# Dot products of the modulation's last eight columns move from the FFN's input norm into the mLSTM's stream

## Chip, cores, metric

The kernel runs on one core of one Trainium2 chip. The metric is the device time of one launch in microseconds (us), the median of three timed runs. The engines are named as in the profile: PE (TensorE, matmuls), DVE (VectorE), ACT (ScalarE), POOL (GpSimd), SP (SyncE, which issues nearly all DMA transfers).

## What is computed

One encoder layer for 1024 tokens of width 1024 in float32. Of it, what matters here:

```python
cond = jax.nn.silu(c)
mod = cond @ w_ada[l] + b_ada[l]
sh1, sc1, g1, sh2, sc2, g2 = jnp.split(mod, 6, axis=-1)
h = modulate(rms_norm(x, norm_mix_g[l]), sh1, sc1)
proj = h @ w_in[l]
...
mix = jnp.concatenate([y_attn, y_mem], axis=-1) @ w_out[l]
x = x + g1[:, None, :] * mix
h = modulate(rms_norm(x, norm_ffn_g[l]), sh2, sc2)
ffn = (jax.nn.silu(h @ w_gate[l]) * (h @ w_up[l])) @ w_down[l]
x = x + g2[:, None, :] * ffn
return rms_norm(x, final_norm_g)
```

`mod` has 6 x 1024 values, kept as 48 columns of 128: columns 0 to 15 are sh1 and sc1, 16 to 39 are g1, sh2 and sc2, and 40 to 47 are g2. g2 is used only where the FFN's output is added, at the end of the layer.

## The kernel before

**Modulation.** A column of `mod` is a dot product of 128 rows of the transposed `w_ada` with `cond`, done on DVE: `cond` (silu of c) lies in all partitions, a half row tile `ada` (128x512, 256 KB) is loaded, and one `scalar_tensor_tensor` multiplies it by `cond` and sums along the row into `modacc`. On the chip that is two instructions, the product and a `DVE_READ_ACCUMULATOR`. `ada_late(last, ahead)` issues the next half column (there are 64 halves for columns 16 to 47), as long as fewer than `ahead` are under way; after the last it calls `mod_sum(40, 48)`, two small additions.

**Stages.** (1) norm 1 and columns 0 to 15; (2) the input projection and the attention, with columns 16 to 39; (3) the mLSTM: four heads, each with state sums (`states`, tiles U, Cs), scores (`front`, tiles E, W), numerators (`back`, na, ni, num) and an end (`last`, `transposed`, tiles hs, ss, dn), as four streams on PE; the rest of the projection (matmuls into `acct`, evacuated by ACT as `vstg`) and then the output projection (`out_unit`, "o" units of the attention and "m" units of the mLSTM) fill PE between them; (4) the last "m" units, whose sums are added into the residual stream by DVE (`x<-acc,mod,x`), squared by ACT (`sq`) and summed by DVE (`ssq`); PE then sums over partitions (`ms`), ACT and DVE make the reciprocal root (`ny`, `nv`), DVE multiplies (`x<-x,ny`), ACT modulates, and ACT, DVE and POOL split the result into high and low parts (`h111h`, `h111l`, ...) and into their sums for the FFN; (5) the FFN in Winograd's form, gate and up, then down; (6) the last norm.

**What sets the order.** All engines' instructions are written in one pass in Python. `Clock` holds the expected end of each engine's work; `Clock.streams` takes the first PE stream that is ready by these expected times, so each expected cost on DVE, ACT, POOL or DMA moves where PE's instructions stand in their order. Once written, every engine works through its own list in order. SP issues DMA transfers in the order of the list too, and an issue that waits for its tile to be free holds up the issues behind it.

Before the change, `cond` is loaded a second time and columns 40 to 47 are made in stage 4, beside the output projection's last units:

```python
        cond_ok = load_cond(PP["ada"])
        ck.streams([un], stop=lambda: cond_ok.done and ada_late(64, 4))
        while not summed:
            ck.need(*adas[-2:])
            ada_late(64, 4)
```

Every vector, scalar and GpSimd instruction goes through the helper `Engine`, so all of them have line 96 in the profile and are told apart by their tiles. Matmuls of three parts (high x high, high x low, low x high) are lines 295 to 297, DMA issues line 300.

Of the kernel before, what the change touches and what calls it, by code (L numbers as in the profile page):

```python
# [20 lines left out]
P = 128  # L21
S = 1024
D = 1024
# [46 lines left out]
class Flag:  # L70
    """done: what sets it is emitted; t: when that is expected to end"""
# [12 lines left out]
class Engine:  # L84
    """An engine's instructions with their expected times."""
# [39 lines left out]
class Clock:  # L125
    """Emits instructions in the order of expected times (us), each engine's in the order in which they are ready."""

    def __init__(self):
        self.t = self.now = self.fin = self.dma_t = self.dma_q = 0.0
        self.q = []  # L130
        self.n = 0
        self.free = {"act": 0.0, "dve": 0.0, "gps": 0.0}
        self.table = "exp"

# [8 lines left out]
    def chain(self, delay, *steps, flag=None, bg=None):  # L143
        """Functions that follow one another. bg: the engine of each step; the step waits until that is idle."""
# [24 lines left out]
    def dma(self, nbytes, issue):  # L169
        """delay until a transfer that is issued now has arrived"""  # L170
# [9 lines left out]
    def need(self, *flags):  # L180
        """What sets the flags is emitted before what follows."""
        for f in flags:
            while not f.done:
                self.pop()
            self.until(f.t)
# [10 lines left out]
    def add_pe(self, dt):  # L196
        """work of the tensor engine that is not a stream's"""
# [7 lines left out]
    def streams(self, mains, fills=(), stop=None):  # L205
        """Runs streams, the first that is ready first, until the mains have ended or stop() holds."""
        every = [*mains, *fills]
        while any(s.wait is not None for s in mains) and not (stop and stop()):
            s = next((s for s in every if s.ready() <= self.t), None)
            if s:  # L210
                s.go()
# [9 lines left out]
class Stream:  # L221
    """A part of the tensor engine's work: a generator that yields the flags that its next piece needs."""
# [15 lines left out]
def layer_kernel(ctx, tc, xT, c, w_ada, vecs, cons, rope, w_f, w_t0, w_t, w_o, w_gu, w_d, out):  # L238
# [8 lines left out]
    # ---------------------------------------------------------------- constants  # L247
# [23 lines left out]
    # DRAM scratch  # L271
# [39 lines left out]
    def psum_open(name, tags, bufs=1):  # L311
        """tags: name -> (tag, buffers)"""
# [7 lines left out]
    class slot:  # L320
        """what frees the next tile of a tag"""
# [26 lines left out]
    with tc.manual_schedule():  # L348
# [12 lines left out]
        def load_cond(pool):  # L361
            """silu of c, the same for all partitions"""
# [11 lines left out]
        # ---------------------------------------------------- weights in a ring of six pieces  # L374
# [46 lines left out]
        def raw(shape, src, flag, arrived):  # L421
            """a transfer into the ring of three; flag: it has been used; arrived(tile, delay)"""
# [10 lines left out]
        def split(p, delay, src, shape, *before, lo=None):  # L433
            """the parts of a piece"""
# [12 lines left out]
        def piece(i):  # L447
            """a piece; its transfer, where it has one of its own"""
# [11 lines left out]
        def load_piece():  # L460
            """the next piece, once there is room for it"""
# [17 lines left out]
        # ---------------------------------------------------- norm 1, modulation, first three tiles  # L479
# [13 lines left out]
        for k in range(KT):  # L493
            def sum_up(k=k):
                """adds a tile's squares"""
# [34 lines left out]
        def rstd_steps(ms, scale, tag, put, flag=None):  # L530
            """1/sqrt(scale*ms + eps), with one Newton step"""
# [25 lines left out]
        def h_steps(k):  # L557
            """the modulated norm of a tile and its parts"""
# [22 lines left out]
        def h_when(k):  # L581
            """starts a tile when its columns of the modulation are there"""
# [26 lines left out]
        # ---------------------------------------------------- q and k: gain, mean square, rotation  # L609
# [6 lines left out]
        def rope_steps(i, accs):  # L616
            """i: q tile 0..3, or 4 for k"""
# [77 lines left out]
        # ---------------------------------------------------- units of the projection  # L695
# [3 lines left out]
        def tile_mms(w0, last):  # L699
            """two halves of a tile of features; last(n, acc, flag) when half n is summed"""  # L700
# [26 lines left out]
        def conv_unit(i, w0):  # L727
# [19 lines left out]
            def silu():  # L747
                """2*silu(y) = y*(1 + tanh(y/2))"""
# [60 lines left out]
        # ---------------------------------------------------- gate rows: fw heads at 0..3, bw heads at 32..35  # L809
        def gate_steps():  # L810
# [100 lines left out]
            def decay():  # L911
                # decay of a chunk: exp(rend + mprev), spread over all partitions
# [19 lines left out]
        def ada_late(last=48, ahead=2):  # L932
            """the next half of a column of the modulation that is not needed at once"""
# [1127 lines left out]
```

## Time and profile before

| | us |
|---|---|
| median of 3 timed runs | 1436.59 |
| lowest, highest | 1433.66, 1437.8 |
| span of the profiled execution, first to last instruction | 1431.8 |
| PE busy | 1310.1 (91%) |
| DVE busy | 1075.9 (75%) |
| POOL busy | 792.6 (55%) |
| ACT busy | 660.6 (46%) |

The profiled execution's own time is known by its span alone; the timed runs lie 1.9 to 6.0 us above that span, the median 4.8. Busy shares are averages over stages that have different limits, so the argument goes by stretches of the span: stage 3 is about 508 to 668 us, stage 4 about 668 to 800, the FFN from there on. A time in brackets at the end of a row is the idle time of that engine just before the instruction, and what ended it.

### The profile page before, as it was taken

What the parts mean: (1) busy time and instruction counts of PE and PEld (TensorE: products, weight loads), DVE (VectorE), ACT (ScalarE), POOL (GpSimd) and SP (SyncE); (2) the same over time, 40 slices, a digit from 0 to 9 for tenths busy, and PEclk for the clock granted to TensorE, in tenths of its full rate; (3) what the DMA queues carried; (4) which work ended last, traced back from release to release, by engine and by line L of the source; (5) the groups of instructions that cost most, each with busy time, mean ns of one, the idle gap of its engine ahead of it and who ended that gap; (6) DMA issues with size and microseconds to landing.
All of it is one profiled execution on the core that took longest, in us unless ns stands there. A gap on an engine that the chain in (4) does not pass through costs nothing.

```text
span 1431.8 us, 19550 instructions
## 1 busy us (share of the span) xinstructions
PE 1310.1 (91%) x6594; PEld 1075.7 (75%) x6602; DVE 1075.9 (75%) x1542; ACT 660.6 (46%) x1191; POOL 792.6 (55%) x624
## 2 busy tenths in 40 slices
PE   5789799999999999899877899999999999979997
PEld 2577677888878988777655688888888887757786
DVE  6947989987788836776899786766666654988676
ACT  5444326677666645454555333332333234433462
POOL 5555454444444336766557564554544444799942
PEclk9899899999999999999999999999999999999999
DMA  7446452322112144824742342232333159623324
GB/s 285 158 127 198 148 153 78 118 66 77 44 52 60 38 136 127 291 94 165 239 155 67 102 141 103 96 106 101 111 110 102 62 185 339 247 67 88 103 63 151
DMA packets 103172, 184.40 MB, mean 129 GB/s; under 512 B 11296, under 2 KB 32672, under 8 KB 103072
## 3 DMA queue, kind: packets, MB, share of 16 engines
q1 hardware_dynamic: 89968, 161.06, 35.2%
q10 hardware_dynamic: 13104, 22.10, 4.2%
q8 instruction: 52, 0.85, 0.3%
q14 instruction: 48, 0.39, 0.1%
HBM read 136.19 MB, written 43.25 MB: 125 GB/s over the span
## 4 chain that ended last, share of the span: by engine, by line
PE 55%; DVE 19%; issue 8%; DMA 7%; POOL 6%; ACT 3%; SPq 1%; DVEq 0%; POOLq 0%; ACTq 0%
PE acc L296 13%; PE acc L295 13%; PE acc L297 13%; POOL wlo L96 3%; DVE x L96 3%; DVE ada L96 3%; DVE sst L96 3%; PE av L1025 2%; DMA wst<-act_d 2%; PE T L1006 2%; DVE PT L96 2%; PE S L974 2%; DVE y L96 2%; PE acct L295 2%; PE acct L297 1%
## 5 line engine op out<-in xcount | busy, mean ns | idle before, releaser
L96 POOL TENSOR_TENSOR wlo<-wst,whi 128x512 fp32r<-128x512 f32 (+2 forms) x208 | 309.0, 1492 | 227.4 <-ACT whi L96 211.2
L96 ACT ACTIVATE whi<-wst 128x512 fp32r<-128x512 f32 (+2 forms) x219 | 131.9, 606 | 141.8 <-PE acc L297 22.4
L96 POOL TENSOR_SCALAR P<-P,sst 128x1024 f32<-128x1024 f32 x64 | 88.9, 1392 | 141.2 <-DVE sst L96 99.8
L296 PE MATMUL acc<-x,whi 128*128 128x512 f32 x352 | 139.6, 397 | 3.3 <-DVE x L96 3.3
L96 POOL TENSOR_TENSOR wlo<-wr,whi 128x512 fp32r<-128x512 f32 x60 | 83.5, 1392 | 78.3 <-ACT whi L96 74.9
L295 PE MATMUL acc<-hh,whi 128*128 128x512 f32 x224 | 97.8, 436 | 13.5 <-ACT hh L96 11.3
L297 PE MATMUL acc<-whi,wcl 128*128 128x512 f32 x244 | 98.1, 402 | 9.5 <-POOL wcl L96 9.5
L96 ACT ACTIVATE P<-S,sst,colq 128x1024 f32<-128x1024 f32 x64 | 77.3, 1207 | 52.2 <-DVE sst L96 47.8
L295 PE MATMUL acc<-whi,wch 128*128 128x512 f32 x244 | 96.8, 397 | 4.0 <-ACT wch L96 4.0
L296 PE MATMUL acc<-hl,whi 128*128 128x512 f32 x224 | 92.8, 414 | 8.2 <-POOL hl L96 4.5
L296 PE MATMUL acc<-wlo,wch 128*128 128x512 f32 x244 | 96.9, 397 | 1.1 <-POOL wlo L96 1.1
L297 PE MATMUL acc<-hh,wlo 128*128 128x512 f32 x224 | 91.5, 409 | 0.0
L96 DVE SCALAR_TENSOR_TENSOR ada<-ada,cond 128x512 f32<-128x512 f32 (+1 forms) x79 | 84.9, 1082 | 7.3 <-DMA ada<-in_w_ada_dram 7.2
L96 DVE TENSOR_TENSOR sg<-acc,sg 128x512 f32<-128x512 f32 x67 | 45.4, 687 | 59.3 <-PE acc L297 58.9
L96 ACT ACTIVATE PT<-T 128x512 fp32r<-128x512 f32 x128 | 71.4, 597 | 37.8 <-PE T L1006 37.1
L96 DVE TENSOR_TENSOR PT<-T,PT 128x512 fp32r<-128x512 f32 x128 | 82.8, 681 | 7.2 <-ACT PT L96 7.1
L96 ACT ACTIVATE whi<-wr 128x512 fp32r<-128x512 f32 x60 | 37.9, 632 | 106.1 <-DVE wr L96 49.6
L96 POOL TENSOR_TENSOR wlo<-s,whi 128x512 fp32r<-128x512 f32 x44 | 60.8, 1383 | 38.3 <-ACT whi L96 31.7
L295 PE MATMUL acct<-whi,hh 128*128 128x256 f32 (+1 forms) x256 | 79.3, 310 | 2.4 <-ACT xp L96 1.0
L296 PEld LDWEIGHTS acc<-x,whi 128*128 128x128 f32 x352 | 66.5, 189 | 19.2 <-DVE x L96 4.2
L96 DVE SCALAR_TENSOR_TENSOR x<-acc,mod,x 128x512 f32<-128x512 f32 (+1 forms) x92 | 62.7, 719 | 24.1 <-PE acc L297 24.1
L1006 PE MATMUL T<-con,P 128*128 128x128 f32 x512 | 70.2, 275 | 10.4 <-DVE PT L96 7.6
(457 smaller groups left out, 3875.1 us busy)
## 6 DMA issues: line engine op xcount, KB each, us to landing
wr<-in_w_gu_dram SPq DMA_DIRECT2D x66, 256.0 KB, 2.8
ada<-in_w_ada_dram SPq DMA_DIRECT2D x64, 256.0 KB, 3.6
wd<-in_w_d_dram SPq DMA_DIRECT2D x22, 512.0 KB, 7.0
wst<-in_w_gu_dram SPq DMA_DIRECT2D x34, 256.0 KB, 3.1
wst<-act_d SPq DMA_DIRECT2D x33, 256.0 KB, 4.1
ada<-in_w_ada_dram SPq DMA_DIRECT2D x16, 512.0 KB, 4.9
wst<-in_w_o_dram SPq DMA_DIRECT2D x32, 256.0 KB, 4.3
act_d<-sg ACTq DMA_DIRECT2D x31, 256.0 KB, 2.0
```

The source lines that it names most:

```text
L96: return fn(*args, **kw)
L295: nc.tensor.matmul(acc, w[0], x[0], start=first, stop=False)
L296: nc.tensor.matmul(acc, w[0], x[1], start=False, stop=False)
L297: nc.tensor.matmul(acc, w[1], x[0], start=False, stop=last)
L974: nc.tensor.matmul(sp[:, halves(n)], qs[:, j * P:(j + 1) * P], k2[g][m][:, halves(n)], start=m == 0, stop=m == 1)
L1006: nc.tensor.transpose(tp[:, k], Pt[q][:, (4 * b + k) * P:(4 * b + k + 1) * P], ident)
L1025: nc.tensor.matmul(av, va[:, k, h // 4], PT[it][m][:, k], start=(k, m) == (0, 0), stop=(k, m) == (NJ - 1, 1))
```

## The change

The condition is loaded, and its silu taken, at the beginning of the mLSTM (stage 3); `ada_late` is called each time `Clock.streams` lets a PE stream go on, with two halves under way at most instead of four, until the 16 halves are done; the two loops of stage 4 lose their calls. The pool of stage 4 that held `cond` and the `ada` tiles is gone; they lie in the pool `big` now. Comments and docstrings are removed as well, which changes no instruction; line numbers behind the additions shift by a few.

```diff
@@ class Clock
+        self.tick = None
...
             s = next((s for s in every if s.ready() <= self.t), None)
             if s:
+                if self.tick:
+                    self.tick()
                 s.go()
                 continue
...
@@ layer_kernel
         kvpool.__exit__(None, None, None)
-        bp = big_open(3)
+        bp = PP["ada"] = big_open(3)
+        load_cond(bp)
...
         mem = [Stream(g) for g in (ends(), backs(), fronts(), all_states())]
+        ck.tick = lambda: ada_late(64)
         ck.streams(mem, [un], stop=lambda: un.wait is None and all(f.done for v in vo_ok for f in v))
+        while not summed:
+            ck.need(*adas[-2:])
+            ada_late(64)
+        ck.tick = None
...
         psum_open("ps3", {"acc": ("acc", 8), "ms": ("acc", 8)})
-        adpool = tc.tile_pool(name="ad", bufs=1, side="right")
-        PP["ada"] = adpool.__enter__()
-        cond_ok = load_cond(PP["ada"])
-        ck.streams([un], stop=lambda: cond_ok.done and ada_late(64, 4))
-        while not summed:
-            ck.need(*adas[-2:])
-            ada_late(64, 4)
-        adpool.__exit__(None, None, None)
+        ck.streams([un])
         opool.__exit__(None, None, None)
```

How the order of instructions moves, at three places. First DVE's list at the beginning of the mLSTM, right after `mod_sum(16, 40)`; `W` are the weights of a score tile, `Cs` the states, `num` the numerators. Before:

```order
L96 SCALAR_TENSOR_TENSOR sc_5005<-mod,vec 128x8
L96 SCALAR_TENSOR_TENSOR W<-tr,W 128x256 x2
L96 SCALAR_TENSOR_TENSOR Cs<-Cs,dec,U 128x130 x4
L96 SCALAR_TENSOR_TENSOR W<-tr,W 128x256 x2
L96 SCALAR_TENSOR_TENSOR Cs<-Cs,dec,U 128x130 x3
L96 SCALAR_TENSOR_TENSOR Cs<-Cs,dec 128x130 x4
```

And with the change:

```order
L96 SCALAR_TENSOR_TENSOR sc_5007<-mod,vec 128x8
L96 SCALAR_TENSOR_TENSOR ada,modacc<-ada,cond 128x512 x3
L96 SCALAR_TENSOR_TENSOR Cs<-Cs,dec,U 128x130 x2
L96 SCALAR_TENSOR_TENSOR W<-tr,W 128x256 x2
L96 SCALAR_TENSOR_TENSOR ada,modacc<-ada,cond 128x512
L96 SCALAR_TENSOR_TENSOR Cs<-Cs,dec,U 128x130 x2
L96 SCALAR_TENSOR_TENSOR W<-tr,W 128x256 x2
L96 SCALAR_TENSOR_TENSOR ada,modacc<-ada,cond 128x512 x2
L96 SCALAR_TENSOR_TENSOR Cs<-Cs,dec,U 128x130 x3
L96 SCALAR_TENSOR_TENSOR Cs<-Cs,dec 128x130 x2
L96 SCALAR_TENSOR_TENSOR ada,modacc<-ada,cond 128x512
```

Three products stand ahead of the first state update and the rest between updates; the sixteenth stands before the second head's third state update, and from there on DVE's list in the mLSTM holds none.

Second, SP's list at the same place, from the first load of the mLSTM on (`mq`, `mk`, `v` are a head's q, k and v, `wst` weights). Before:

```order
L300 DMA mq<-mqk_d_85 128x256
L300 DMA mk<-mqk_d_89 128x1024
L300 DMA v_5017<-v_d_93 128x8x128
L300 DMA v_d_94<-vstg 128x256 x2
L300 DMA wst<-in_w_t_dram 128x512 x2
```

And with the change:

```order
L303 DMA cond<-in_c_dram 128x1024
L303 DMA ada<-in_w_ada_dram 128x512
L303 DMA mq<-mqk_d_85 128x256
L303 DMA ada<-in_w_ada_dram 128x512
L303 DMA mk<-mqk_d_89 128x1024
L303 DMA v_5023<-v_d_93 128x8x128
L303 DMA v_d_94<-vstg 128x256
L303 DMA wst<-in_w_t_dram 128x512
L303 DMA ada<-in_w_ada_dram 128x512
L303 DMA wst<-in_w_t_dram 128x512
```

The condition and two halves are issued ahead of the head's k and v, and further halves between the weights; the third half's issue waits for the first product to free its tile.

Third, DVE's list in stage 4, from the sum of squares after the first reciprocal root to the low part `h113l` that PE needs. Before:

```order
L96 TENSOR_TENSOR x_6177<-x_6177,ny 128x512
L96 SCALAR_TENSOR_TENSOR x_5973<-acc,mod,x_5973 128x512
L96 TENSOR_TENSOR h111l<-x_6071,h111h 128x512
L96 SCALAR_TENSOR_TENSOR ada,modacc<-ada,cond 128x512 x2
L96 SCALAR_TENSOR_TENSOR x_5982<-acc,mod,x_5982 128x512
L96 SCALAR_TENSOR_TENSOR ada,modacc<-ada,cond 128x512
L96 TENSOR_TENSOR ssq<-ssq,sq 128x512
L96 TENSOR_TENSOR mod<-modacc,vec 128x8
L96 TENSOR_TENSOR mod<-mod,modacc 128x8
L96 SCALAR_TENSOR_TENSOR x_6008<-acc,mod,x_6008 128x512
L96 TENSOR_TENSOR h113l<-x_6099,h113h 128x512
```

And with the change:

```order
L96 TENSOR_TENSOR x_6234<-x_6234,ny 128x512
L96 SCALAR_TENSOR_TENSOR x_6033<-acc,mod,x_6033 128x512
L96 TENSOR_TENSOR h111l<-x_6122,h111h 128x512
L96 SCALAR_TENSOR_TENSOR x_6045<-acc,mod,x_6045 128x512
L96 TENSOR_TENSOR ssq<-ssq,sq 128x512
L96 TENSOR_TENSOR h113l<-x_6168,h113h 128x512
```

The products and the two additions of `mod_sum(40, 48)` are gone from between the norm's steps; one addition of a tile's sum (`x<-acc,mod,x`) that stood ahead of `h113l` now stands behind it.

## Rows read from the trace of the kernel before

**Rows 1.** The page: span, and the busy time of each engine.

```profile
span 1431.8 us, 19550 instructions
...
PE 1310.1 (91%) x6594; PEld 1075.7 (75%) x6602; DVE 1075.9 (75%) x1542; ACT 660.6 (46%) x1191; POOL 792.6 (55%) x624
```

**Rows 2.** Busy time by stretch: from and to, length, then busy us (and instructions) of PE, PE's weight loads, DVE, ACT and POOL, the granted clock of PE, the share of the DMA engines, GB/s. The last line is of the FFN.

```profile
508.00:520.00 12.00, 10.20 (x78) 9.38 (x79) 1.05 (x4) 2.68 (x8) 1.91 (x9) 1.00 0.61 196
520.00:540.00 20.00, 19.94 (x145) 18.85 (x145) 10.44 (x32) 11.13 (x34) 10.82 (x21) 1.00 0.41 124
540.00:560.00 20.00, 19.89 (x148) 18.82 (x149) 11.58 (x30) 12.41 (x33) 15.32 (x26) 1.00 0.38 120
...
600.00:620.00 20.00, 16.20 (x85) 13.83 (x86) 16.06 (x34) 7.91 (x22) 11.80 (x17) 0.91 0.45 147
...
640.00:660.00 20.00, 19.74 (x103) 16.36 (x103) 16.45 (x36) 9.35 (x23) 14.11 (x11) 1.00 0.42 138
...
720.00:740.00 20.00, 13.01 (x43) 9.51 (x42) 17.77 (x28) 8.83 (x15) 6.82 (x5) 0.83 0.56 185
...
760.00:780.00 20.00, 14.40 (x46) 10.05 (x44) 20.00 (x18) 8.84 (x17) 15.04 (x10) 0.83 0.13 42
780.00:800.00 20.00, 12.57 (x43) 9.18 (x44) 15.18 (x16) 8.36 (x16) 15.47 (x11) 0.83 0.28 90
...
900.00:1000.00 100.00, 100.00 (x435) 81.38 (x434) 67.22 (x79) 31.08 (x50) 50.14 (x37) 1.00 0.31 106
```

**Rows 3.** DVE's groups of one shape: count, busy us, mean ns of one, idle us before them. The first line is of the stretch 675 to 730, the second of 698 to 730, the last two of 520 to 560 and of 560 to 600.

```profile
L96 DVE SCALAR_TENSOR_TENSOR ada<-ada,cond 128x512 f32<-128x512 f32 x16 | 17.7, 1118 | 0.1
...
L96 DVE SCALAR_TENSOR_TENSOR ada<-ada,cond 128x512 f32<-128x512 f32 x8 | 9.8, 1230 | 0.0
...
L96 DVE SCALAR_TENSOR_TENSOR Cs<-Cs,dec 128x130 f32<-128x130 f32 x7 | 2.5, 353 | 0.3 <-ACT Cs L96 0.2
...
L96 DVE SCALAR_TENSOR_TENSOR Cs<-Cs,dec 128x130 f32<-128x130 f32 x8 | 8.2, 1021 | 0.3
```

**Rows 4.** The chain of work that ended last, in the stretch 686 to 730 (44 us): shares of the stretch by engine, tile and line. "issue" is time in which the engine waited for nothing that the profile shows.

```profile
by line: DVE x L96 22.0%; DVE ada L96 21.4%; DVE ssq L96 17.7%; issue 13.7%; PE acc L296 5.2%; PE ms L1159 4.7%; PE acc L295 3.5%; PE acc L297 3.5%; ACT sq L96 2.9%; DVE ny L96 1.6%; DVE nv L96 1.6%; DVE h113l L96 1.4%; DVE h111l L96 1.4%; 
```

**Rows 5.** What PE waited for in the stretch 695 to 735: us in total, times, longest.

```profile
PE acc L296 <- DVE h113l L96: 4.7, 1, 4.7
PE ms L1159 <- DVE ssq L96: 3.3, 1, 3.3
PE acc L296 <- DVE h111l L96: 2.3, 1, 2.3
```

**Rows 6.** PE's instructions in order of time (start, us, what) around these waits. There are eleven matmuls between the last two lines.

```profile
691.57 0.39 PE L297 MATMUL acc<-yah,wlo 128*128 128x512 f32 x1
695.26 2.08 PE L1159 MATMUL ms<-ssq,ones 128*128 128x512 f32 x2 [3.30 <-DVE ssq L96]
...
719.87 0.39 PE L295 MATMUL acc<-h110h,whi 128*128 128x512 f32 x1
...
724.53 0.40 PE L295 MATMUL acc<-h113h,whi 128*128 128x512 f32 x1
729.62 0.79 PE L296 MATMUL acc<-h113l,whi 128*128 128x512 f32 x1 [4.69 <-DVE h113l L96]
730.21 0.63 PE L297 MATMUL acc<-h113h,wlo 128*128 128x512 f32 x1
...
735.29 0.39 PE L297 MATMUL acc<-h113h,wlo 128*128 128x512 f32 x1
```

**Rows 7.** DVE's and ACT's instructions in order of time, in stage 4.

```profile
692.85 0.74 DVE L96 SCALAR_TENSOR_TENSOR x<-acc,mod,x 128x512 f32<-128x512 f32 x1
...
693.68 0.63 ACT L96 ACTIVATE sq<-x 128x512 f32<-128x512 f32 x1 [3.51 <-DVE x L96]
...
694.52 0.68 DVE L96 TENSOR_TENSOR ssq<-ssq,sq 128x512 f32<-128x512 f32 x1
...
701.94 0.75 DVE L96 SCALAR_TENSOR_TENSOR x<-acc,mod,x 128x512 f32<-128x512 f32 x1 [1.44 <-PE acc L297]
...
728.88 0.68 DVE L96 TENSOR_TENSOR h113l<-x,h113h 128x512 fp32r<-128x512 f32 x1
...
739.36 0.69 DVE L96 TENSOR_SCALAR nv<-ms 128x512 f32<-128x512 f32 x1 [2.20 <-ACT ny L96]
```

**Rows 8.** The beginning of the mLSTM in order of time: PE's first transposition of k, and DVE's first work after 508.3.

```profile
515.63 0.41 PE L1675 MATMUL tr<-con,mk 128*128 128x128 f32 x2 [1.43 <-issue]
...
518.76 0.76 DVE L96 SCALAR_TENSOR_TENSOR W<-tr,W 128x256 f32<-128x256 f32 x2 [10.43 <-DMA v_d<-vstg]
```

**Rows 9.** What PE waited for on DVE in the mLSTM; the first line is of the stretch 508 to 580, the second of 600 to 668.

```profile
PE ni L1787 <- DVE num L96: 1.8, 2, 1.0
...
PE ni L1787 <- DVE num L96: 5.5, 2, 3.7
```

**Rows 10.** The silu of the condition on ACT in stage 4, with the table load ahead of it, and the transfer of the condition: KB, us from issue to landing.

```profile
673.88 1.28 ACT L96 ACT_TABLE_LOAD   x1
675.18 1.06 ACT L96 ACTIVATE cond<-cond 128x1024 f32<-128x1024 f32 x1
...
cond<-in_c_dram SPq DMA_DIRECT2D x1, 512.0 KB, 4.6
```

## Prediction

> **What bounds the kernel now.** The page comes first: PE is busy for 91% of 1431.8 us [rows 1], so most of the span is PE's. The busy times by stretch say where it is not [rows 2]. In the FFN (900 to 1000) PE is busy all the time: what stage 4 gains or loses reaches the end unchanged. In the first part of the mLSTM (520 to 560) PE is busy 39.8 of 40 us, DVE 22.0, so PE bounds and DVE has 18 us to spare. In stage 4 it is the other way round: PE is busy 13.0, 14.4 and 12.6 us in the three stretches of 20 from 720, 760 and 780, DVE 17.8, 20.0 and 15.2, and PE's granted clock is 0.83 there. The chain that ended last agrees: between 686 and 730 two thirds is DVE, and 21.4% of these 44 us, **9.4 us**, are the sixteen products' own [rows 4]. Their mean there is 1118 ns [rows 3]. The change takes them out of that place.
>
> **What it takes out of stage 4.** Sixteen products, 17.7 us of DVE [rows 3], their accumulator reads, a table load and the silu on ACT, 1.28 and 1.06 us [rows 10], and 4.7 MB of transfers. I look at it from PE and from DVE.
>
> From PE: it waited 2.3 us for `h111l` and 4.7 for `h113l` [rows 5]. DVE worked without a gap from 701.94 to the end of `h113l` at 729.56, 27.6 us [rows 7]. Of the eight products between 698 and 730 seven lie in this stretch, at the mean of 1.23 us 8.6 [rows 3]. Without them `h113l` ends at 701.94 + 19.0 = 720.9, and PE asks for it at about 724.8, after the matmul that starts at 724.53 [rows 6]. Both waits, **7.0 us**, go, with almost 4 us to spare; the change also puts one addition of a sum behind `h113l`. After the second wait the twelve matmuls from 730.21 to 735.29 took 0.63 us each at first against 0.39 at the end [rows 6]: PE ran at 1.2 instead of 2.4 GHz, and half of these 5.1 us, **2.5**, comes back if PE doesn't stop. The wait of 3.3 us before `ms` shrinks little: the last sum of the unit ahead ends at 691.96, the addition, the square and the addition of squares need 0.74 + 0.63 + 0.68 = 2.05 [rows 6, 7], with some 0.3 between them 694.3 instead of 695.26, **1.0**. PE's sum is 10.5.
>
> From DVE: the chain's 9.4 us go, but the two products ahead of `ms` (about 2.7 of them) give only the 1.0 just worked out, since PE's last sum then sets the time: 9.4 - 2.7 + 1.0 = **7.7**. From 739.36, where DVE starts on the second root after an idle time of 2.2 us [rows 7], to about 793 DVE sets the pace [rows 2], so the smaller sum counts. Above it stands up to 1.4 more, the wait of DVE for PE at 701.94 [rows 7], if PE's slow clock after `ms` goes too. I take **8**, with 5 and 11 as bounds: 5 if POOL's work, freed of DVE's, moves so that other DVE instructions meet it, 11 if PE's sum is reached.
>
> The transfers freed from 674 to 726 and the table load cost the path nothing now: PE's waits there are on DVE alone [rows 5].
>
> **What it adds to the mLSTM.** The products take DVE time from about 514 on, in DVE's list until the second head's third state update. That is about 555 in the trace of before. DVE is busy 1.05 us in 508 to 520 and 22.0 in 520 to 560 [rows 2]; with 17.7 it would be 41 of 52. PE has the projection's matmuls to fill with, but PE's list is fixed, so a state or numerator that is late by more than the list allows stops PE, with everything behind it. Price: where DVE was busy 16.1 and 16.5 of 20 us, in 600 to 660, about as full as it will be here, PE waited 5.5 us for `num`; at half the load, 1.8 in 72 us [rows 2, 9]. The order was written with the products' expected time in it, so the lists already give way. Two or three microseconds of new waits are near the middle of these rows. Against that stands a gap that closes: PE waited 1.43 us ahead of the first transposition of k [rows 8], and the changed list has 24 more projection matmuls in front of it, at 145 matmuls in 19.94 us [rows 2] about 3.3 us of work, which are merely done earlier. Net I take **1 us lost**; the bounds are a gain of 1.4 and a loss of all 19 us of DVE time.
>
> The condition's transfer and its silu: SP issues them ahead of the head's k and v. The condition took 4.6 us to land [rows 10]; issued at about 508.3, where DVE's idle time of 10.4 us begins [rows 8], it has its silu done by about 514, ahead of the 518.76 at which DVE starts. One half (256 KB) ahead of k and v costs 1.3 us at the 196 GB/s of this stretch [rows 2]; the 3.3 us of projection matmuls cover it. What this costs if that cover is gone is the 1.3 us. ACT gets the silu and two table loads, 1.06 + 2 x 1.28 = 3.6 us, in a stretch where it is busy 2.7 of 12 [rows 2, 10]; behind it waits the evacuation of the two `acct` sums, with PE behind that. I cost it at nothing, 1 us at most.
>
> On the table load page and trace differ. The row has the silu start 1.30 us after the load began, so a load costs 1.3 [rows 10]. The Trainium skill, "ScalarE: Activation LUTs", section "What ACT_TABLE_LOAD costs", adds a drain of about 1.38 us to the 1.28, some 2.66 for each switch. By that, ACT would be held 6.4 us instead of 3.6 at the beginning of the mLSTM, PE would stop for its two sums, and the sum would be about 2.8 us worse; the trace shows no such drain.
>
> **Sum.** Stage 4 gives 8, the mLSTM costs 1: the span goes from 1431.8 to 1424.8. The median lies 4.8 above the span of the profiled execution, so **1429.6 us**, 0.5% faster.
>
> **Rivals.** *Slower: the mLSTM pays.* DVE's small state updates stretch when POOL works: 353 ns in 520 to 560, 1021 in 560 to 600 [rows 3]. The products, 128x512, hold DVE for 0.7 to 1.8 us at a time in the middle of the chain of states, which DVE does one after the other. If 60% of their 19 us became PE waits, 11.4, less the 8 of stage 4, that is 3.4 slower, 1440; it decides from 42% on. For it: the products' mean of 1118 ns, and that PE's list is rigid. Against it: 1.8 us of PE waits for DVE in 508 to 580, and DVE's 29 idle us of 52. The Trainium skill, "GPSIMD Engine Reference", section "Key points", says that GpSimd shares its SBUF interfaces with VectorE and contends with instructions of two SBUF inputs, as the products are; by that rule they stay slow in the new place, where POOL is busy 26 of 40 us, and POOL's own work stretches too. The two means of the state update agree.
>
> *No change: stage 4 doesn't follow.* DVE's time is given back to POOL's and ACT's: the high parts come from ACT, the low parts partly from POOL, and the products lay in gaps. Then only the `ms` wait and the slow clock go, 1.0 + 2.5, less the 1: 1434. For it: 13.7% of the chain is issue [rows 4]. Against it: both long waits name DVE.
>
> *More: both slow-clock stretches go and the mLSTM costs nothing.* 10.5 + 1.4 = 12: 1424.7.
>
> **How the numbers follow.** Chances: the forecast 0.47, more 0.15, no change 0.20, slower 0.18. About 0.3%, 4.3 us, is what a measurement can tell. The forecast and "more" are faster by more than that: 0.62; 0.20 the same; 0.18 slower. The range goes from 1423.5 (stage 4 at its upper bound of 11, the gap closed, 12.4, and some scatter) to 1439, most of the way to the slower case, with about 2 in 10 outside.
>
> **What the changed profile would show.** Right: no wait of PE for `h111l` and `h113l` of over 1 us; no stretch at 0.63 us per matmul after them; DVE in 508 to 560 busy near 38 of 52 us with PE still above 95% there; the span from the first `ms` to the first full FFN stretch shorter by about 7. Wrong: PE waits for `num`, `U` or `Cs` between 515 and 600 that sum to over 5 us; SP waiting for a product while k, v or weights stand behind it; or the same waits in stage 4 put down to ACT or POOL instead of DVE.

## The result, and the profile after

The changed kernel takes **1425.07 us** (median of 6 runs, 1424.10 to 1430.91) against 1435.12 before (6 runs). The ratio of the runs on record is 0.9949, 95% interval 0.9928 to 0.9970; it is an estimate of its own and not the quotient of the two medians, which is 0.9930. The kernel is faster by 0.5%; the forecast was 1429.6, in a range of 1423.5 to 1439. Beside the experiments it ran once more: 1427.12 (6 runs), ratio 0.9937 (0.9922 to 0.9953). Over both, twelve runs have a median of 1426.2 and lie up to 7 us apart; the runs of some other kernels below lie up to 11 us apart.

The profile shown here is of the run of 1430.91 us. Its span and its busy times, from the page:

```profile
span 1429.1 us, 19533 instructions
...
PE 1312.8 (92%) x6602; PEld 1079.3 (76%) x6602; DVE 1078.9 (75%) x1542; ACT 660.8 (46%) x1192; POOL 792.5 (55%) x624
```

DVE has as much work as before [rows 1]; it lies elsewhere. In this profile the modulation's first addition, the last thing ahead of the mLSTM, starts at 510.81; in that of before at 507.75, and in the second profile of the changed kernel at 506.76. Those 3 to 4 us belong to the run and not to the change, so the table counts from that addition. Each number is the start of an instruction in the trace less the start of `mod<-modacc,vec`: the first transposition of `hs` (the end of the mLSTM's first head), the two `ms` matmuls of the norm, and the first matmul on `hT40h` in the FFN.

| us after the addition | first hs | first ms | second ms | hT40h |
|---|---|---|---|---|
| before | 39.0 | 187.5 | 229.8 | 301.4 |
| changed | 46.9 | 188.6 | 220.1 | 294.0 |
| changed, second profile | 46.6 | 187.4 | 218.7 | 293.1 |

To the first `hs` the changed kernel is 8 us behind, at the first `ms` level, and at `hT40h` 7 to 8 us ahead. The second `ms` isn't at the same place in PE's two lists: in the changed kernel it stands twelve matmuls earlier, as rows further down show. So the third column compares two different points, and from the first `ms` to `hT40h` is the stretch to go by: 113.9 us before, 105.4 and 105.7 now. Now the views that answer to the rows of before. Busy time by stretch (columns as in [rows 2]):

```profile
508.00:560.00 52.00, 46.28 (x349) 43.50 (x348) 31.61 (x90) 25.55 (x69) 23.68 (x42) 1.00 0.64 201
...
700.00:720.00 20.00, 20.00 (x86) 15.97 (x85) 17.90 (x20) 15.65 (x27) 11.63 (x9) 1.00 0.40 125
720.00:740.00 20.00, 14.25 (x52) 10.42 (x51) 17.55 (x19) 8.40 (x16) 10.79 (x7) 0.83 0.62 207
...
760.00:780.00 20.00, 13.07 (x40) 8.97 (x39) 20.00 (x17) 8.80 (x15) 16.55 (x10) 0.83 0.09 32
```

In 508 to 560 PE was busy for 50.0 of 52 us before and is for 46.3 now, DVE for 23.1 before and 31.6 now [rows 2]; in the second profile it is 47.4 and 34.0. In 700 to 720 PE is busy throughout; in 760 to 780 DVE is full, as before.

The products on DVE in the mLSTM (508 to 562; columns as in [rows 3]), the chain that ended last in 690 to 735, and what PE waited for in 690 to 735:

```profile
L96 DVE SCALAR_TENSOR_TENSOR ada<-ada,cond 128x512 f32<-128x512 f32 x16 | 12.8, 809 | 11.9 <-DMA ada<-in_w_ada_dram 6.4 <-DMA mq<-mqk_d 5.5
```

```profile
by line: DVE x L96 31.6%; DVE ssq L96 18.2%; DMA wr<-in_w_gu_dram 12.5%; issue 8.0%; PE ms L1162 7.1%; ACT sq L96 4.3%; DVE nv L96 3.1%; SPq L303 2.7%; DVE h111l L96 2.3%; PE acc L300 2.1%; PE acc L299 2.1%; PE acc L298 2.1%; ACT ny L96 1.5
```

```profile
PE ms L1162 <- DVE ssq L96: 6.4, 2, 5.8
```

The products take 12.8 us where they took 17.7 [rows 3]; their 21.4% of the chain in stage 4 [rows 4] is gone. The 12.5% for `wr`, weights of the FFN that DVE reads, lie at 724.3 to 729.9; DVE's timeline has no idle time there, so DVE didn't stop for this transfer. Of PE's three waits [rows 5] those for `h111l` and `h113l` are gone, and `ms` has the one that is left. Instructions in order of time (PE, then DVE):

```profile
698.39 0.39 PE L300 MATMUL acc<-yah,wlo 128*128 128x512 f32 x1
699.44 1.12 PE L1162 MATMUL ms<-ssq,ones 128*128 128x512 f32 x2 [0.66 <-DVE ssq L96]
700.00 0.80 PE L298 MATMUL acc<-yah,whi 128*128 128x512 f32 x1
700.64 0.39 PE L299 MATMUL acc<-yal,whi 128*128 128x512 f32 x1
...
722.36 0.45 PE L299 MATMUL acc<-h113l,whi 128*128 128x512 f32 x1
...
724.73 0.40 PE L300 MATMUL acc<-h112h,wlo 128*128 128x512 f32 x1
730.88 2.07 PE L1162 MATMUL ms<-ssq,ones 128*128 128x512 f32 x2 [5.75 <-DVE ssq L96]
731.97 1.42 PE L298 MATMUL acc<-h113h,whi 128*128 128x512 f32 x1
733.18 0.63 PE L299 MATMUL acc<-h113l,whi 128*128 128x512 f32 x1
```

```profile
697.20 0.74 DVE L96 SCALAR_TENSOR_TENSOR x<-acc,mod,x 128x512 f32<-128x512 f32 x1
698.70 0.69 DVE L96 TENSOR_TENSOR ssq<-ssq,sq 128x512 f32<-128x512 f32 x1 [0.76 <-ACT sq L96]
...
703.41 0.75 DVE L96 SCALAR_TENSOR_TENSOR x<-acc,mod,x 128x512 f32<-128x512 f32 x1 [0.74 <-PE acc L300]
...
721.58 0.68 DVE L96 TENSOR_TENSOR h113l<-x,h113h 128x512 fp32r<-128x512 f32 x1
...
730.15 0.68 DVE L96 TENSOR_TENSOR ssq<-ssq,sq 128x512 f32<-128x512 f32 x1
```

Before, the second `ms` stood behind the last product of `h212h`, twelve matmuls further on:

```profile
737.34 0.40 PE L297 MATMUL acc<-h212h,wlo 128*128 128x512 f32 x1
737.58 1.02 PE L1159 MATMUL ms<-ssq,ones 128*128 128x512 f32 x2
```

The first `ms` waits 0.66 us instead of 3.30, and the matmuls behind it take 0.39 to 0.40 from the second on, where eight took 0.63 in the trace of before. From the first `ms` to the second it is now 31.4 us, 42.3 before. Then DVE is what PE waits for again: the last sum of squares ends at 730.83, PE waits 5.75 us for it, and behind that wait the matmuls take 0.63 us (the granted clock is 0.50, 1.2 GHz, in 731 to 734). From the second `ms` to `hT40h` it takes 73.9 us against 71.6; that isn't a loss, since the twelve matmuls that stood ahead of `ms` are behind it now.

### The profile page after: what moved, and what is told of

Same layout as the page of the kernel before. It is cut to its first block, busy times and chain, and to the rows that moved or that the text cites. A ratio compares the mean times of both kernels' runs of the same rounds, so it can differ in the third digit from the quotient of the medians.

```text
span 1429.1 us, 19533 instructions
## 1 busy us (share of the span) xinstructions
PE 1312.8 (92%) x6602; PEld 1079.3 (76%) x6602; DVE 1078.9 (75%) x1542; ACT 660.8 (46%) x1192; POOL 792.5 (55%) x624
## 4 chain that ended last, share of the span: by engine, by line
PE 54%; DVE 21%; issue 8%; DMA 6%; POOL 5%; ACT 4%; SPq 1%; DVEq 0%; ACTq 0%; POOLq 0%
PE acc L299 13%; PE acc L300 13%; PE acc L298 13%; DVE x L96 4%; DVE ada L96 3%; POOL wlo L96 3%; DVE sst L96 3%; PE av L1028 2%; PE T L1009 2%; DVE PT L96 2%; DVE y L96 2%; PE S L977 2%; PE acct L298 2%; PE acct L300 1%; PE acct L299 1%
## 5 line engine op out<-in xcount | busy, mean ns | idle before, releaser
L96 POOL TENSOR_TENSOR wlo<-wst,whi 128x512 fp32r<-128x512 f32 (+2 forms) x208 | 304.9, 1471 | 212.1 <-ACT whi L96 190.0
L96 DVE SCALAR_TENSOR_TENSOR ada<-ada,cond 128x512 f32<-128x512 f32 (+1 forms) x79 | 79.0, 1008 | 19.6 <-DMA ada<-in_w_ada_dram 14.1
L96 DVE TENSOR_REDUCE sst<-S 128x1 f32<-128x1024 f32 x64 | 77.7, 1214 | 1.8 <-PE S L977 1.6
```

The costliest lines, as they stand in the source:

```text
L96: return fn(*args, **kw)
```

## The experiments

Each row is one kernel; the ratio is to the kernel before on the same chip, with its 95% interval. The three columns on the right count from the modulation's addition, as above, in the kernel's one profile.

| kernel | median us | ratio | first hs | first ms | hT40h |
|---|---|---|---|---|---|
| changed, again | 1427.1 | 0.9937 (0.9922 to 0.9953) | 46.6 | 187.4 | 293.1 |
| none | 1424.6 | 0.9932 (0.9914 to 0.9950) | 39.0 | 184.9 | 290.4 |
| stage4_loads | 1424.6 | 0.9938 (0.9914 to 0.9961) | 40.1 | 189.9 | 294.4 |
| stage4_products | 1434.6 | 1.0010 (0.9992 to 1.0027) | 38.4 | 187.0 | 300.9 |
| stage4_twice | 1444.2 | 1.0075 (1.0053 to 1.0098) | 39.1 | 193.2 | 310.8 |
| mlstm_loads | 1423.9 | 0.9939 (0.9917 to 0.9960) | 45.9 | 185.4 | 290.5 |
| mlstm_twice | 1432.3 | 0.9981 (0.9968 to 0.9994) | 52.7 | 192.5 | 297.2 |
| resident | 1439.6 | 1.0024 (1.0010 to 1.0039) | 44.5 | 199.7 | 304.3 |
| resident_same_order | 1425.6 | 0.9948 (0.9932 to 0.9963) | 45.0 | 185.9 | 290.9 |
| resident_loads | 1437.7 | 1.0026 (1.0010 to 1.0041) | 43.6 | 199.7 | 304.7 |
| att | 1429.6 | 0.9959 (0.9945 to 0.9973) | 39.7 | 182.1 | 286.8 |
| att_loads | 1423.8 | 0.9933 (0.9911 to 0.9955) | 40.7 | 180.2 | 284.9 |

**The changed kernel again.** No edit.

> The changed kernel once more, beside the kernels below on the same chip, for a second profile. The time is expected at 1425, between 1424 and 1431, and faster than before by 0.5%. My theory (DVE's time in the input norm) expects in its profile what the first showed: no wait of PE for h111l and h113l over 1 us, and from the second ms to the first operand hT40 some 7 us less than before. The first profile began stage 3 about 3 us later than the profile of before, ahead of any changed instruction; this one is expected to show whether that belongs to the change (again 3 us) or to the run (near 0).

Measured: 1427.1; the addition at 506.76, so the 3 us belonged to the run.

**None of it: what is there to gain.**

```diff
-        bp = PP["ada"] = big_open(3)
-        load_cond(bp)
+        bp = big_open(3)
...
-        ck.tick = lambda: ada_late(64)
+        dve.tensor_copy(mod[:, 40:48], V("b_ada", 40, 8))
...
```

> The changed kernel without the sixteen products, their transfers and the second load of the condition: columns 40 to 47 are left at their bias, a part of the modulation that is not computed. It tells what the products cost where they are now. My theory, that the mLSTM pays about 1 us, expects 1424, at most 2 below the changed kernel. The rival, that the mLSTM pays much and that the gain of stage 4 is larger than I worked out, expects 4 to 8 us below it: 1417 to 1421, with the start of the mLSTM (from the first addition of the modulation to the first transposition of k, to the first U and to the first hs) shorter by about that much.

Measured: 1424.6. PE's list of this kernel is that of before up to stage 4; in stage 4 the second `ms` stands twelve matmuls earlier, as in the changed kernel, and DVE, ACT and POOL have some of their instructions in another order. The two kernels differ by stage 4 alone: 10.6 us by the medians, and by the profiles 2.6 ahead of the first `ms` and 8.4 from there to `hT40h`, together 11.0. From this bound the changed kernel is 1.6 us away by the medians (1426.2) and 2.5 to 3.7 at the first `ms`, by its two profiles. The rival with a dear mLSTM and a larger gain falls.

**Which half of stage 4's load counts.** The transfers stay, the products go; and the other way round.

```diff
 # stage4_loads
...
-            adas.append(ck.chain(dma(t, w_ada[j][:, halves(i)]), lambda: dve.scalar_tensor_tensor(
+            adas.append(ck.chain(dma(t, w_ada[j][:, halves(i)]), (
+                (lambda: ck.run("dve", 0.07 + 1.05 / 2)) if n >= 48 else lambda: dve.scalar_tensor_tensor(
 # stage4_products
+            else:
+                t, arrive = kept[48 + n % 4], ck.dma(P * HALF * 4, 0.5)
```

> The kernel before, with the condition, its silu and the sixteen transfers still in the input norm, but without the products: columns 40 to 47 are left at their bias. The expected costs stay in the planner, so that every engine's list is that of before but for the sixteen products. If DVE's time is what the change freed (my theory), this is as fast as the kernel without any of it: 1425, and from the first ms to hT40 it takes 105 to 106 us instead of 114. If the 4.2 MB of transfers in that place cost the time (the rival), it stays at 1434 to 1435.

> The other half: the kernel before with the sixteen products in the input norm, done on four half tiles that are loaded once and used over and over, so that twelve of the sixteen transfers are gone (the values of columns 42 to 47 are not those of the reference). The planner is told the same times. My theory expects no change against before, 1435 within 2 us, and 113 to 114 us from the first ms to hT40. The rival, transfers, expects 1426 to 1428.

Measured: 1424.6 without the products, 1434.6 with them and without twelve of the transfers. What PE waited for in 690 to 735 in these two kernels:

```profile
PE acc L296 <- DVE h113l L96: 2.5, 1, 2.5
PE ms L1160 <- DVE ssq L96: 2.1, 2, 1.4
```

```profile
PE acc L296 <- DVE h113l L96: 4.7, 1, 4.7
PE ms L1165 <- DVE ssq L96: 3.5, 1, 3.5
PE acc L296 <- DVE h111l L96: 2.3, 1, 2.3
```

The products alone reproduce the waits of [rows 5] to 0.2 us, and the transfers cost nothing that the medians show. The cause is DVE's time, and not a new order: in stage4_loads PE's, ACT's and POOL's lists are those of before row for row, and DVE's is too but for the products and the two additions behind them. From the first `ms` to `hT40h` it takes 104.5 us, 9.4 less than before. Two longer waits of PE are left in this kernel, 2.50 us for `h113l` and 1.45 for the second `ms`, which stands where it stood before. PE's rows, and under them DVE's addition that waits for PE, and `h113l`:

```profile
698.32 1.12 PE L1160 MATMUL ms<-ssq,ones 128*128 128x512 f32 x2 [0.67 <-DVE ssq L96]
...
724.05 0.50 PE L296 MATMUL acc<-h113l,whi 128*128 128x512 f32 x1 [2.50 <-DVE h113l L96]
...
731.11 1.12 PE L1160 MATMUL ms<-ssq,ones 128*128 128x512 f32 x2 [1.45 <-DVE ssq L96]
```

```profile
702.28 0.75 DVE L96 SCALAR_TENSOR_TENSOR x<-acc,mod,x 128x512 f32<-128x512 f32 x1 [0.73 <-PE acc L297]
...
722.82 1.17 DVE L96 TENSOR_TENSOR h113l<-x,h113h 128x512 fp32r<-128x512 f32 x1
```

The profile of stage4_loads reached its first `ms` 5 us later than that of `none`, though their medians are equal. In it the granted clock is 0.50 in 672 to 677, ahead of the first `ms`, where the profiles of before and of `none` have 1.00; one profile is one run.

**Stage 4's cost doubled.**

```diff
-            adas.append(ck.chain(..., lambda: dve.scalar_tensor_tensor(...)))
+            adas.append(ck.chain(..., lambda: (n >= 48 and nc.vector.scalar_tensor_tensor(...),
+                dve.scalar_tensor_tensor(...))))
```

> The kernel before with each of the sixteen products in the input norm done twice, the planner charged once. 17.7 us more of DVE in that place. Taking the products out gave about 10.5 us to hT40 for 17.7 us of DVE. If DVE sets the pace there, the second product costs at least what the first did, 10 to 18 us: 1444 to 1452. If the products lay in gaps of DVE and the gain came from something else that went with them, less than 4 us: up to 1438.

Measured: 1444.2, 8.8 above the median of before, a little under the theory's lower end; by the ratio it is 10.8 (7.6 to 14.1). The two sets of products on DVE (675 to 740):

```profile
L96 DVE SCALAR_TENSOR_TENSOR ada<-ada,cond 128x512 f32<-128x512 f32 x16 | 15.8, 989 | 0.6
L942 DVE SCALAR_TENSOR_TENSOR ada<-ada,cond 128x512 f32<-128x512 f32 x16 | 15.0, 937 | 0.0
```

Together 30.8 us, 13.1 more than the 17.7 of one set [rows 3], not 17.7 more: the products of both sets are shorter on average than the 1118 ns of one set alone. `hT40h` comes 9.4 later. So in stage 4 a microsecond of products costs 0.5 to 0.6 (9.1 by stage4_loads and 10.6 by `none`, of 17.7, the first set) to 0.7 (9.4 of 13.1, the second) at the end.

**The mLSTM's cost taken away, and doubled.** The first has the edit of stage4_loads, made in the changed kernel, the second that of stage4_twice.

> The changed kernel with the condition, its silu and the transfers in the mLSTM, but without the sixteen products there (columns 40 to 47 at their bias); the planner keeps the expected costs, so PE's list is the changed kernel's but for one place. It tells whether the mLSTM pays with DVE's time or at SP and ACT. The kernel with none of it needed 184.9 us from the modulation's addition to the first ms, the changed kernel 187.4. If DVE's products are what costs these 2.5 us, this one needs 185 and the time is 1424.5; if the load of the condition, the table loads and the transfers ahead of k and v cost them, it needs 187.4 and the time is 1426 to 1427.

> The changed kernel with each of the sixteen products in the mLSTM done twice (the second overwrites the first's sum, and columns 40 to 47 are not those of the reference), and the planner charged once, so that only DVE's list differs. It doubles the cost that is in dispute: 16 x 0.81 = 12.9 us more of DVE. Without the products the mLSTM needed 185.4 us to the first ms, with them 187.4. If DVE has room there, as I costed it, the second product costs as much as the first, 2 us: 1428. The rival, that DVE is nearly full (18.9 of 20 us in 540 to 560), expects most of the 12.9 us at the end: 1434 to 1438.

Measured: 1423.9 and 1432.3. What PE waited for in 508 to 620 without the products, and its waits on DVE of over 1 us with the products done twice:

```profile
PE ni L1791 <- DVE num L96: 4.4, 2, 3.4
PE na L1786 <- ACT whi L96: 2.8, 1, 2.8
PE tr L1679 <- DMA v_d<-vstg: 1.1, 1, 1.1
```

```profile
PE ni L1792 <- DVE num L96: 4.6, 4, 2.2
PE U L1708 <- DVE Cs L96: 3.2, 3, 1.4
...
PE tr L1853 <- DVE dn L96: 1.6, 1, 1.6
```

Without products the 7 us of delay to the first `hs` are still there (45.9) and are made up by the first `ms` (185.4 against 184.9 of `none`). So that delay comes with the new order and the loads, in which projection work stands ahead of the mLSTM's, and is nearly free. What the first set of products costs isn't clear of the scatter: 2.0 at the first `ms` (3.2 by the changed kernel's other profile), 2.3 by the medians, and between nothing and 1.4 by the ratios (0.9939 without, 0.9937 and 0.9949 with them). If 2.3 is right, it is 0.2 for a microsecond of products (12.8 us). The second set is clear: 5.1 at the first `ms` and 6.1 by the median, 0.4 to 0.5 for a microsecond (12.5 and 13.1 us for the two sets, 25.6 in all). Neither theory had that: there is more room for one set than for two, and what gives way first is `Cs`, the states, on which PE waited for 0.4 us at most with one set. The wait for `num` isn't new: in 508 to 620 it is 5.5 us before and in `none`, 4.0 and 5.6 in the changed kernel.

**The condition kept on chip.**

```diff
-            cond = PP["cond"] = pool.tile([P, D], F32, name="cond", bufs=1)
+            cond = PP["cond"] = mid.tile([P, D], F32, name="cond", bufs=1)
...
         bp = PP["ada"] = big_open(3)
-        load_cond(bp)
 # resident_same_order, in place of the last line
+        arrive = ck.dma(P * D * 4, 0.5)
+        ck.chain(arrive, silu_cost)
```

> The changed kernel with the condition kept on chip from stage 1 on: no second load, no second silu and no table loads at the start of the mLSTM; the products stay in the mLSTM. My theory costed the reload at nothing: 1425, within 1 us of the changed kernel. The rival, that the load and the table load stand on the path to the first k and to the first W (PE waited 1.7 us for v's store and 2.8 us for the high parts of W in the changed kernel), expects 2 to 4 us less: 1421 to 1423.

> The condition kept on chip, as in the run that came out at 1439.6, but with the planner charged for the transfer and the silu that are not issued, so that PE's, DVE's and POOL's lists are the changed kernel's word for word, and only SP's one transfer, ACT's silu and the table loads are gone. If that run was slow because its lists were ordered otherwise (655 of 5771 rows of PE's list differ), this one is at 1424 to 1426, and from the modulation's addition to the first hs it needs 2 to 3 us less than the changed kernel's 46.6. If the place of the condition in memory is at fault, it is at 1437 to 1440 again.

> The slow kernel with the condition kept on chip and lists of its own order (1439.6), without its sixteen products, whose transfers and expected costs stay (columns 40 to 47 at their bias): PE's, ACT's, POOL's and SP's lists are the same. It tells whether that order is slow by itself or because of the products' time in it. If by itself, the first ms is again 199 to 200 us after the modulation's addition and the time 1437 to 1440. If the products make it slow, the first ms is at 185 to 188 and the time 1424 to 1427. My theory of a list that gives way to the products says the first: the waits that cost there, 5.8 us for num and 5.5 for the high part of the attention's output, stand at 647 to 700, 90 us behind the last product.

Measured: 1439.6, 1425.6 and 1437.7. Both theories of the first run fell: less work made the kernel 13 us slower (1439.6 against 1426.2). The second gives the reason as far as it goes: with the changed kernel's lists the condition may lie on chip, and the time is the changed kernel's. The third has the slow order without the products and is as slow, with the same two waits at the same places. These are its waits of PE in 640 to 700; the first run has 5.8 for `num` and 5.5 for `yah` there, the changed kernel 0.5 and 0.2:

```profile
PE ni L1791 <- DVE num L96: 6.6, 2, 5.8
PE acc L298 <- ACT yah L96: 5.4, 1, 5.4
```

So it is the order by itself. The planner was told of one transfer and one silu less, put 655 of 5771 rows of PE's list elsewhere, and ended in a list in which PE stops for the last numerators. Which of those rows does it wasn't tried. The reload itself costs 1.5 us at the first `ms` (187.4 against 185.9) and 0.6 by the medians, which is no more than their scatter.

**All of it in the attention.**

```diff
-        def ada_late(last=48, ahead=2):
+        def ada_late(last=64, ahead=2):
...
-        while len(adas) < 48:
+        while len(adas) < 64:
...
-        mod_sum(16, 40)
+        mod_sum(16, 48)
...
```

> All 64 half columns in the attention, none in the mLSTM or in stage 4; the condition is still on chip there, so it isn't loaded again. The products in the attention took 0.68 us each (median of 20) against 1.12 in stage 4, and after the present 48 halves, from 300 us on, DVE is busy 29 of 40 us and PE 39 to 40. If DVE's time in the input norm is the cause of the gain, as my theory has it, it is kept here in full and the mLSTM pays nothing: 1423, 1 to 4 us below the changed kernel. The rival, that DVE's time counts in the attention as it did in stage 4, expects 11 us (16 products of 0.68) given back there: 1434.

> The kernel with all 64 half columns in the attention, again without the last sixteen products (their transfers stay, columns 40 to 47 are at their bias), with the planner charged for them, so that PE's, ACT's, POOL's and SP's lists are the same. That kernel came out at 1429.6, and its attention ended 12 to 14 us later (the modulation's addition at 520.6 instead of 507 to 508). If DVE's time in the attention is what this costs, the addition is back at 508 to 511 and the time 3 to 10 us less, 1420 to 1426. If it is the changed order of the lists, the addition stays at 519 to 521 and the time at 1429.

Measured: 1429.6, and 1423.8 without the products. Busy time in 295 to 375 of these two:

```profile
295.00:375.00 80.00, 75.84 (x507) 68.02 (x506) 67.15 (x131) 52.81 (x96) 39.61 (x30) 0.98 0.35 109
```

```profile
295.00:375.00 80.00, 77.62 (x537) 70.36 (x534) 59.34 (x106) 53.74 (x99) 37.15 (x32) 1.00 0.36 108
```

With DVE busy 59 of 80 us and PE 77.6, the products (14.1 us for sixteen, 0.89 each) still cost 5.8 us by the medians and 3.7 by the ratios, at most 0.4 for a microsecond: PE does 30 matmuls less in these 80 us. The modulation's addition starts at 515.6 without and 520.6 with them, 5.0 apart. That the addition is late without them too comes from the new order and the transfers, which weren't taken apart. More of the work is done ahead of it: from there to `hT40h` the kernel needs 284.9 us, 5.5 less than `none`, and the two times agree within 1 us. Neither my theory (free) nor its rival (all 11 us) came out; the cost lies between them.

## Why the prediction was right, point by point

**Stage 4's bound: right, but not by the waits I named.** Products alone give the waits of before, transfers alone do not. In the changed kernel PE's two long waits are gone, and that DVE sets the pace to the second root shows in PE's new wait of 5.75 us for the second `ms`. With the lists of before, though (stage4_loads), the wait for `h113l` only shrinks, from 4.69 to 2.50, and 1.45 for `ms` is new. PE comes earlier there too, so the 7.0 us of waits did not go "with almost 4 us to spare". `h113l` ends 25.7 us behind the start of the first `ms` in that kernel (723.99 less 698.32), 34.3 before, and the working's 720.9 is 25.6 behind it. That this agrees is luck: DVE's addition that waits for PE comes 4.0 behind the first `ms` and not 6.7 (702.28 there, 701.94 before), and from it to the end of `h113l` it takes 21.7 and not 19.0.

**Its size: under-estimated, 8 for 10.6 to 11.** Two terms were too small. The wait ahead of the first `ms` was to shrink by 1.0, and it shrank by 2.6 (3.30 to 0.66; 0.72 in `none`, whose PE list is that of before up to this place). I took the unit that PE finishes last ahead of `ms` for the one that `ssq` sums. The rows of after show that it isn't: PE's last matmul of that unit starts at 698.39, while the `x` that `ssq` needs is made at 697.20. DVE was late by its own products, not by PE. The other term is the slow clock behind that wait. From the start of `ms` to the tenth matmul behind it are 5.7 us before and 3.1 now, and DVE's addition that waits for this work of PE starts 6.7 us behind the first `ms` before (701.94) and 4.0 now (703.41). I had 1.4 for it, and only in the rival. The third term came out: from the first `ms` to `hT40h` stage4_loads gains 9.4, and less the 2.7 of the clock that is 6.7, as much as my 9.4 less the 2.7 of the two products ahead of `ms`. Luck has a part in it, for I read the chain's 9.4 us as the sixteen products, and only twelve of them lie in 686 to 730. In the changed kernel the same stretch gains 8.2 to 8.5. The 2.5 us of the slow clock behind `h113l` did not come back there: the slow stretch moved behind the second `ms`. The whole, 10.6 to 11, is PE's sum of 10.5 and not DVE's 7.7, but a new wait of 5.75 us stands against the 7.0 of waits that PE's sum counts.

**The mLSTM: a size not settled.** 1 us lost was forecast; it is 2.5 to 3.7 at the first `ms` by the profiles and 1.6 by the medians against `none`, and the products' own part is not clear of the scatter. What I looked for there came otherwise: DVE busy 31.6 and 34.0 of 52 and not 38, mostly since a product takes 0.81 there and not 1.1; PE at 89 and 91% and not above 95%, for waits on k or v (1.7 and 0.8) and on ACT (2.8, put down to `whi`, with the second table load just ahead in ACT's list). The wait on ACT is there without the products too (mlstm_loads), and without the table loads it is 1.6, for `Cs` (resident_same_order). Two signs that I had set down as wrong came or nearly came: PE's waits for `num`, `U` and `Cs` in 515 to 600 are 3.0 and 5.1 us in the two profiles, 1.8 before, and SP waited 8.9 us for products, 4.2 at the longest, with weights and q behind it. Neither shows that the products are dear: without them the waits for `num` there are still 3.4 us (mlstm_loads), so most of that comes with the new order and the loads. The 3.3 us of projection matmuls that were to cover the half tile ahead of k and v are real and more than that: the first `hs` is 7.6 to 7.9 us late and the first `ms` is level with that of before.

**ACT: right.** In the trace after, ACT's table loads at the start of the mLSTM:

```profile
514.50 1.28 ACT L96 ACT_TABLE_LOAD   x1
515.79 1.06 ACT L96 ACTIVATE cond<-cond 128x1024 f32<-128x1024 f32 x1
...
523.99 1.28 ACT L96 ACT_TABLE_LOAD   x1
525.29 1.14 ACT L96 ACTIVATE W<-E,cols 128x128 f32<-128x128 f32 x4
```

Each time the next instruction starts 1.29 to 1.30 us after the load, as in [rows 10]. The Trainium skill, "ScalarE: Activation LUTs", section "What ACT_TABLE_LOAD costs", adds a drain of some 1.38 us; no row here shows it, and taking both loads and the silu away moved the median by 0.6 us, less than the scatter.

**The rivals.** *Slower* had a mechanism that is there, with the wrong weight: it needed 42% of DVE's time as PE waits, and the first set of products cost at most 18% (2.3 of 12.8); the second set, at 40% or more, is that rival. Its argument from POOL holds by half: single products took up to 1.69 us in the mLSTM, but their mean is 0.81 there and 1.12 in stage 4. The Trainium skill, "GPSIMD Engine Reference", section "Key points", has VectorE's instructions of two SBUF inputs contend with GpSimd. The trace agrees in stage 4; which of the two engines is stretched differs in the mLSTM, as the last section shows. *No change* fell with stage4_loads. *More*, at 1424.7, was nearest in time. Of its parts the clock behind the first `ms` came; the slow stretch further on only moved, and a free mLSTM is not shown.

**The sum.** 8 less 1 was 7. It was 10.6 to 11 less 1.6 to 2.5, so 8.5 to 9. On top of it, the 4.8 us that I added from the profile's span to the median were too much. In every run whose span is on record the time is 1.7 to 1.9 us above the span, so the profiled execution of before took some 1433.6, 3.0 below the median that I started from; and the median of before is 1433.7 to 1435.4 in later sets of 17 to 25 runs, not 1436.6. Both errors point the same way, and the time came out 3 to 5 us below the forecast. It lies within the range, but at the time of *More*, to which I had given 0.15.

## What to carry to other kernels

In this kernel, work that left the engine that bounds a stage gave back 0.5 to 0.7 of its time there; work that came to an engine that is idle half the time cost 0.2 at most, if anything, for a first helping and 0.4 to 0.5 for a second. Before a wait is priced from the instruction that ends last on the other engine, look up which one the waiting instruction reads. Where a planner writes the lists, test a change of work with the lists held fixed: here less work with a new order cost 13 us, and the same work with the old order nothing. A marker in the trace measures a stretch only while it keeps its place in its engine's list.

## What I had not expected of the hardware

The same product, 128x512 from two SBUF operands, took 0.68 to 1.79 us in stage 4 and 0.65 to 2.88 over the whole trace of before: on average 1.12 in stage 4, 0.94 and 0.99 there when done twice, 0.89 in the attention, 0.81 in the mLSTM. Moved, sixteen of them took 4.9 us less DVE time.

What POOL does beside a product sorts these times. In stage 4 of before eight of the sixteen have no POOL instruction beside them and take 0.68 to 0.69 us; the other eight run beside POOL's instructions of two tensors (`wlo<-wst,whi`, `h110l`, `h212l`) and take 1.08 to 1.79. In the mLSTM of the changed kernel nine run beside POOL. Two of them, beside `wlo` and `hs<-hs,so`, take 1.48 and 1.69; the other seven, most of them beside `wv<-v,cols` (one tensor and a column), take 0.68 to 0.80. There POOL is the one that is stretched: four `wv` alone take 1.44 us, three beside two products 3.03. So, as far as these traces tell, the mean fell because the products met other work of POOL's; no run tests this by itself. In stage 4 before (DVE, POOL), and in the mLSTM after:

```profile
691.15 1.77 DVE L96 SCALAR_TENSOR_TENSOR ada<-ada,cond 128x512 f32<-128x512 f32 x1
690.64 3.40 POOL L96 TENSOR_TENSOR wlo<-wst,whi 128x512 fp32r<-128x512 f32 x2
...
695.13 0.68 DVE L96 SCALAR_TENSOR_TENSOR ada<-ada,cond 128x512 f32<-128x512 f32 x1
```

```profile
541.90 1.44 POOL L96 TENSOR_SCALAR wv<-v,cols 128x130 f32<-128x130 f32 x4 [5.27 <-DMA v<-v_d]
...
559.72 0.68 DVE L96 SCALAR_TENSOR_TENSOR ada<-ada,cond 128x512 f32<-128x512 f32 x1
561.02 0.68 DVE L96 SCALAR_TENSOR_TENSOR ada<-ada,cond 128x512 f32<-128x512 f32 x1
559.23 3.03 POOL L96 TENSOR_SCALAR wv<-v,cols 128x130 f32<-128x130 f32 x3
```

And the slow clock follows the longer waits, but not in proportion. Behind the waits of 3.30 and 4.69 us in the trace of before eight and eleven matmuls take 0.63 us, behind that of 5.75 us in the trace after four, and behind the waits of 2.50 and 1.45 us in stage4_loads and of 0.66 us in the trace after none.
